# An MoE bias load on another queue, and a reordered end, in a decoder layer

## The chip, the cores and the metric

The kernel runs on one core of a Trainium2 chip, and the metric is the device time of one execution in microseconds (us). Inside the core, TensorE (PE; its weight loads are PEld), VectorE (DVE), ScalarE (ACT), GpSimd (POOL) and SyncE (SP) each work through a list of their own and wait for each other by semaphores. DMAs are issued by SP and ACT, each from its place in its list, and are carried out by 16 DMA engines that the core has.

## The reference

One decoder layer on 256 tokens of width 1024, all in float32: a mixer with three branches, a LayerNorm, a mixture of experts, a LayerNorm. The change touches the mixture of experts alone:

```
logits = xf @ router_w + router_b
top_v, top_i = lax.top_k(logits, 4)            # 4 of 32 experts for each token
gates = jax.nn.softmax(top_v, axis=-1)
...
def expert_block(xblk, e):
    h = xblk @ w1[e] + b1[e]                   # (., 1024) @ (1024, 2048)
    gate, upv = jnp.split(h, 2, axis=-1)
    gate = jnp.minimum(gate, 7.0); upv = jnp.clip(upv, -7.0, 7.0)
    act = (upv + 1.0) * (gate * jax.nn.sigmoid(1.702 * gate))
    return act @ w2[e] + b2[e]                 # (., 1024) @ (1024, 1024)
...
y = sum over a token's experts of gate * expert_block
x = layer_norm(ALPHA * x + y, ln2_g, ln2_b)
```

The weights of one expert are 12 MB (8 MB of `w1`, 4 MB of `w2`), so 384 MB over 32 experts. The second bias `b2` is 32 x 1024 numbers, 128 KB in all.

## The kernel before, in words

The mixer comes first. Then a loop goes over the experts e = 0 to 30, and the last one, 31, is written out behind it. Each expert works on up to 64 tokens, which a matmul with a matrix of zeros and ones gathers into a token buffer: there are three, `xg[0]` to `xg[2]`, used in turn (expert e uses `xg[e % 3]`), and `xg[2]` lies in the tile `rws`. For an expert, `gemm1` makes the first product into the PSUM tiles `h`, copied into `hs` (in tile `t`) by ACT and DVE; `act_steps` transposes `hs` on PE, adds the first bias while it empties PSUM into `hT`, and then makes the activation `a` with DVE and one sigmoid on ACT. `gemm2` makes the second product from `a`, ACT copies it into `ys`, and `scatter` adds it, weighted by the gates, to four PSUM tiles `acc` that hold the sum over all experts. The loop runs these staggered: within the body of expert e stand gemm1 and act of e, gemm2 of e-1, and scatter of e-2 or e-1. The second bias enters once for all: `gated_biases` adds the gates (transposed, tile `GT`) times the rows of `b2` to `acc`, four products of 512 columns.

The weights stream through a ring of 23 buffers of 1 MB (`new_w`, tile `w`). `load_w` (L75) issues one load of 1 MB from SP: eight for a `w1`, four for a `w2`. Program order of the loads is: `w1` of expert 0; then for each e, `w1` of e and `w2` of e-1. The last expert's weights are loaded by a class `Last` with some pieces of 512 KB (L1157). The loads are issued from SP's list as far ahead of their use as two things allow: a free buffer of the ring (a wait for PE), and a free semaphore. The framework below the kernel gives every DMA of SP's and ACT's queues, in the order of the program's text, the next of eight semaphores, DMAHW0 to DMAHW7; a DMA waits for the one that held its semaphore before, whichever queue that was on.

In the kernel before, `b2` is loaded by SP in the body of expert 30 into a ring buffer of its own (L1291), and `gated_biases` stands in that body, between the transposes of act and the rest of it. `gates_by_expert` makes `GT` in the body of expert 8. Experts with more than 64 tokens would be finished after the loop by `overflow`, a branch that is taken only when the largest count is above 64.

Of the kernel before, what the change touches and what calls it, by code (L numbers as in the profile page):

```python
# [19 lines left out]
D = 1024  # L20
# [31 lines left out]
def hybrid(ctx: ExitStack, tc: tile.TileContext, A, out, dbg=None):  # L52
# [967 lines left out]

    hs = t1[:, :1024]
    hT = t1[:, 1024:].rearrange("p (j h s) -> p j h s", j=8, h=2)
    wblk = rws.rearrange("p v k e -> p (v k e)")
# [66 lines left out]
    def gemm1(xg, w1):  # L1090

        hp = [h_tile(c) for c in range(2)]
        for k, c, half in w1.order:
            PE.matmul(hp[c][half * 64:(half + 1) * 64], xg[:, k],
                             w1(k, half * 2 + c), start=(k == 0), stop=(k == 7), skip_group_check=True)
        nc.scalar.copy(hs[:, :512], hp[0])  # L1096
        nc.vector.tensor_copy(hs[:, 512:], hp[1])  # L1097

    class Weights:


        def __init__(self, e, one=False):
            self.e, self.one = e, one
            self.order = ([(k, c, half) for c in range(2) for half in range(2) for k in range(8)] if one else
                          [(k, c, half) for k in range(8) for c in range(2) for half in range(2)])

        def block(self, name, k, c):
            cs = slice(c * 512, (c + 1) * 512)
            if name == 'moe_w1':
                src = A[name][ds(self.e, 1), k * 128:(k + 1) * 128, cs]  # L1110
            else:
                src = w2v[ds(self.e, 1), :, k // 2, k % 2, cs]
            nc.sync.dma_start(wblk, src.rearrange("e p f -> p (e f)"))
            return wblk

    class First(Weights):
        def load(self):
            self.w = [load_w(w1v[self.e][:, k:k + 1, :], 1, 2048) for k in range(8)]
            return self

        def __call__(self, k, c):
            if self.one:
                return self.block('moe_w1', k, c)
            return self.w[k][:, 0, c * 512:(c + 1) * 512]

    class Second(Weights):
        def load(self):
            self.w = [load_w(w2v[self.e][:, q], 2, 1024) for q in range(4)]
            return self

        def __call__(self, k, c):
            if self.one:
                return self.block('moe_w2', k, c)
            return self.w[k // 2][:, k % 2, c * 512:(c + 1) * 512]

    class Last:
# [26 lines left out]
                PE.matmul(hp[c][h * 64:(h + 1) * 64], xg[(E - 1) % 3][:, k], w,  # L1163
                          start=(k == 0), stop=(k == 7), skip_group_check=True)

        def second(self, yp, j, c):

            for h in range(2):
                PE.matmul(yp[c][h * 64:(h + 1) * 64, :256], a_main[:, j],
                          self.w2[j // 2][:, j % 2, h * 512 + c * 256:h * 512 + (c + 1) * 256],  # L1170
                          start=(j == 0), stop=(j == 7), skip_group_check=True)

    def act_steps(bias, a, g=None, banks=None):


        bv = bias.rearrange("p (h j) -> p j h", h=2)
        pieces = [slice(q * 4, (q + 1) * 4) for q in range(2)]
        js = slice(0, 8)
        if g is not None:
            js = slice(4 * g, 4 * g + 4)  # L1180
            pieces = [js]
        for i, piece in enumerate(pieces):
            n = piece.stop - piece.start
            p = (banks[i] if banks else u_tile())[:, :n * 128]
            for j in range(n):
                PE.transpose(p[:, j * 128:(j + 1) * 128], pair(hs, piece.start + j), ident)
            nc.vector.tensor_tensor(hT[:, piece], p.rearrange("p (j h s) -> p j h s", j=n, h=2),  # L1187
                                    bv[:, piece, :].unsqueeze(3).to_broadcast([128, n, 2, SLOTS]), op=OP.add)
        yield
        gate, up = hT[:, js, 0, :], hT[:, js, 1, :]  # L1190
        nc.vector.tensor_scalar(gate, gate, LIMIT, None, op0=OP.min)
        sg = hs[:, js.start * 128:js.start * 128 + (js.stop - js.start) * 64].rearrange("p (j s) -> p j s", s=64)
        nc.scalar.activation(sg, gate, AF.Sigmoid, scale=1.702)
        nc.vector.tensor_scalar(up, up, LIMIT, -LIMIT, op0=OP.min, op1=OP.max)
        nc.vector.tensor_tensor(sg, sg, gate, op=OP.mult)
        nc.vector.scalar_tensor_tensor(a[:, js], up, 1.0, sg, op0=OP.add, op1=OP.mult)  # L1196

    def act(*args, **kw):
        for _ in act_steps(*args, **kw):
# [2 lines left out]

    def gemm2(a, w2):
        yp = u_tile()
        for k, c, half in w2.order:
            if c == 0:
                PE.matmul(yp[half * 64:(half + 1) * 64, :], a[:, k], w2(k, half),
                                 start=(k == 0), stop=(k == 7), skip_group_check=True)
        nc.scalar.copy(ys, yp)  # L1209

    def scatter(gT, first=False):
# [7 lines left out]
    def gates_by_expert():  # L1219
        p = u_tile()[:E, :T]  # L1220
        for t in range(2):
            PE.transpose(p[:, t * 128:(t + 1) * 128], G[:, t, :], ident)
        GT = lp.tile([E, T], F32, name="GT")
        nc.vector.tensor_copy(GT, p)
        return GT

    def gated_biases(GT, b2r):
        for t in range(2):
            for h in range(2):
                PE.matmul(acc[t][h], GT[:, t * 128:(t + 1) * 128], b2r[:, h * 512:(h + 1) * 512],  # L1230
                                 start=False, stop=False, skip_group_check=True)

    def overflow(stores):

# [4 lines left out]
        with tc.If(most > SLOTS):  # L1239
            with tc.For_i(0, E, 1) as ei:  # L1240
                ce = nc.values_load(cnts[0:1, ds(ei, 1)], min_val=0, max_val=T)
                with tc.If(ce > SLOTS):
                    be = lp.tile([128, 16], F32, name="be")
                    nc.vector.tensor_copy(be.unsqueeze(2), b1T[:, :, ds(ei, 1)])
                    gev = lp.tile([128, 2, 1], F32, name="gev")
                    nc.vector.tensor_copy(gev, G[:, :, ds(ei, 1)])
                    rke = lp.tile([128, 2, 1], F32, name="rke")
                    nc.vector.tensor_copy(rke, rk[:, :, ds(ei, 1)])
                    with tc.For_i(1, T // SLOTS, 1):
                        nc.vector.tensor_scalar(rke, rke, float(SLOTS), None, op0=OP.subtract)  # L1250
# [3 lines left out]
                        gemm1(xg[0], First(ei, True))  # L1254
                        a = act(be, xg[0])
                        gemm2(a, Second(ei, True))
                        scatter(gT)
            st = row_sums()
            for c in range(2):
# [22 lines left out]
    for e in range(E - 1):  # L1282
# [3 lines left out]
        w1 = First(e).load()  # L1286
        if 0 < e < E - 2:
            w2 = Second(e - 1).load()
        if e == E - 2:
            b2r = new_w()[:E, :D]  # L1290
            nc.sync.dma_start(b2r, A['moe_b2'])  # L1291
        if e:
            weigh(gates(e), buf)
            if e == E - 2:
# [15 lines left out]
        elif e < E - 2:  # L1310
# [13 lines left out]
            if odd:  # L1324
                gT = turn_slots(buf, h_tile(0))
                find(e + 1, 1, u_tile())
            late = prev[1], e == 1
            if e == SUMS:
                scatter(*late)
                late = None  # L1330
                residuals()
                GT = gates_by_expert()
# [28 lines left out]
    steps = [act_steps(b1T[:, :, E - 1], a_main, c) for c in range(2)]  # L1361
    yp = []
    for c in range(2):
        for k in (6, 7):
            last.first(banks, k, c)
        nc.scalar.copy(hs[:, c * 512:(c + 1) * 512], banks[c])
        if c:
            yp.append(h_tile(0))
            for j in (0, 1):
                last.second(yp, j, 0)  # L1370
        next(steps[c])
        for _ in steps[c]:
            pass
    yp.append(h_tile(1))
    for j in range(6):
        for c in range(2):
            if j > 1 or c:
                last.second(yp, j, c)

    def row_sums():  # L1380
        return [lp.tile([128, 4, 6], F32, name=f"st{t}") for t in range(2)]
# [7 lines left out]
    for c in range(2):  # L1389
        cs = slice(c * 256, (c + 1) * 256)  # L1390
        for j in (6, 7):
            last.second(yp, j, c)
        nc.scalar.copy(ys[:, cs], yp[c][:, :256])  # L1393
        for t in range(2):
            for h in range(2):
                r = slice(h * 64, (h + 1) * 64)
# [4 lines left out]
    y = new_w().rearrange("p (t d) -> p t d", t=2)  # L1401

    def normed(st):
        stats = [statistics(st[t]) for t in range(2)]
# [48 lines left out]
```

## Time and profile before

| | |
|---|---|
| device time, median of 3 runs (range) | 1202.81 us (1200.18 to 1204.87) |
| the profiled execution: its own time, its span | 1199.88 us, 1198.0 us |
| PE busy | 1134.0 us (95% of the span) |
| DVE, ACT, POOL busy | 347.0, 208.2, 64.4 us |
| bytes read from HBM | 447.25 MB, 374 GB/s over the span |

The span goes from the first to the last instruction of the profiled execution; about 1.9 us of its time lie around it. The profile cuts the span in 40 equal slices, and from the tenth on it shows the DMA engines filled.

### The profile page before, as it was taken

How to read it: one execution, taken by the hardware profiler on the slowest of the kernel's cores; microseconds unless marked ns; L12 is line 12 of the kernel's file. 1: busy time of each engine (PE TensorE's matmuls, PEld its weight loads, DVE VectorE, ACT ScalarE, POOL GpSimd, SP SyncE). 2: the span in 40 equal slices, each digit the busy share in tenths (PEclk: the TensorE clock that was granted, in tenths of full speed). 3: DMA queues.
4: the chain of work that ended last, by engine and by line, in shares of the span. 5: the costliest groups of instructions: out<-in, count | busy, mean ns of one | idle time of the engine just before them, and what ended most of it. 6: DMA issues, size and time to landing. Idle time of an engine off the chain costs nothing.

```text
span 1198.0 us, 15607 instructions
## 1 busy us (share of the span) xinstructions
PE 1134.0 (95%) x6464; PEld 584.8 (49%) x6465; DVE 347.0 (29%) x700; ACT 208.2 (17%) x491; POOL 64.4 (5%) x106
## 2 busy tenths in 40 slices
PE   8999999999999999999999898989898989899994
PEld 7998889984434334343433333333333333334332
DVE  6679777472112111111121111111111111111014
ACT  5115554532101011010101000101010101011001
POOL 1010001311000000000000000000000000000000
PEclk9999999999999999999999999999999999999998
DMA  9994466869999999999999999999999999999993
GB/s 247 327 321 142 129 205 250 306 231 419 424 424 424 424 425 423 425 423 425 423 425 422 426 423 425 423 424 423 426 423 425 424 424 425 425 424 425 419 406 153
DMA packets 100358, 449.37 MB, mean 375 GB/s; under 512 B 11108, under 2 KB 44826, under 8 KB 51514
## 3 DMA queue, kind: packets, MB, share of 16 engines
q1 hardware_dynamic: 99774, 447.51, 92.6%
q8 instruction: 52, 0.85, 0.3%
q10 hardware_dynamic: 508, 0.81, 0.2%
q14 instruction: 24, 0.20, 0.1%
HBM read 447.25 MB, written 1.05 MB: 374 GB/s over the span
## 4 chain that ended last, share of the span: by engine, by line
DMA 51%; PE 45%; DVE 2%; SPq 1%; ACT 1%; issue 0%; ACTq 0%; DVEq 0%
DMA w<-in_moe_w_dram 50%; PE h L48 16%; PE u L48 8%; PE mm L87 4%; PE mm L88 4%; PE mm L89 4%; PE acc L48 3%; DMA w<-in_w_in_dram 1%; PE sc L641 1%; PE yps L686 1%; PE ptp L677 1%; PE sc L48 1%; PE mm L48 1%; DVE w L48 0%; DMA x<-in_x_dram 0%
## 5 line engine op out<-in xcount | busy, mean ns | idle before, releaser
L48 PE MATMUL h<-w,t 128*64 128x512 f32 (+1 forms) x1472 | 328.0, 588 | 31.2 <-DMA w<-in_moe_w_dram 30.4
L48 PEld LDWEIGHTS h<-w,t 128*64 128x64 f32 x1472 | 99.4, 136 | 249.0 <-issue 161.4
L48 PE MATMUL u<-w,t 128*64 128x512 f32 x960 | 212.9, 595 | 0.0
L1097 DVE COPY t<-h 128x512 f32<-128x512 f32 x31 | 21.4, 691 | 512.8 <-PE h L48 512.8
L48 PE MATMUL h<-w,rws 128*64 128x512 f32 x640 | 146.2, 603 | 11.2 <-DMA w<-in_moe_w_dram 11.0
L48 PEld LDWEIGHTS u<-w,t 128*64 128x64 f32 x960 | 66.2, 137 | 124.4 <-issue 118.3
L48 PEld LDWEIGHTS h<-w,rws 128*64 128x64 f32 x640 | 43.8, 138 | 108.7 <-issue 76.1
L87 PE MATMUL mm<-xh,ws 128*128 128x256 f32 x336 | 96.8, 288 | 0.0
L1096 ACT COPY t<-h 128x512 f32<-128x512 f32 x31 | 18.1, 585 | 447.5 <-PE h L48 447.5
L88 PE MATMUL mm<-xl,ws 128*128 128x256 f32 x336 | 95.0, 283 | 0.0
L89 PE MATMUL mm<-xh,ws 128*128 128x256 f32 x336 | 94.9, 283 | 0.0
L82 DVE TENSOR_TENSOR ws<-w,ws 128x1024 fp32r<-128x1024 f32 (+1 forms) x64 | 73.2, 1148 | 11.8 <-ACT ws L81 11.0
L1074 POOL TENSOR_TENSOR ext<-ext,G 128x128 f32<-128x128 f32 x62 | 27.1, 456 | 815.8 <-PE h L48 797.2
L48 PE MATMUL acc<-t,ext 64*128 64x512 f32 (+1 forms) x264 | 63.9, 602 | 1.6 <-ACT t L1393 0.9
L87 PEld LDWEIGHTS mm<-xh,ws 128*128 128x128 f32 x336 | 64.3, 191 | 1.0 <-issue 0.8
L88 PEld LDWEIGHTS mm<-xl,ws 128*128 128x128 f32 x336 | 64.4, 192 | 0.0
L89 PEld LDWEIGHTS mm<-xh,ws 128*128 128x128 f32 x336 | 64.3, 191 | 0.0
L1196 DVE SCALAR_TENSOR_TENSOR t<-t 128x512 f32<-128x512 f32 (+1 forms) x32 | 21.6, 675 | 144.0 <-PE u L48 143.8
L1209 ACT COPY t<-u 128x512 f32<-128x512 f32 x31 | 18.2, 586 | 175.3 <-PE u L48 175.3
L1187 DVE TENSOR_TENSOR t<-u,b1T 128x512 f32<-128x512 f32 x35 | 24.0, 690 | 78.3 <-PE u L48 78.3
L48 PEld LDWEIGHTS acc<-t,ext 64*128 64x128 f32 x264 | 22.7, 186 | 41.1 <-issue 27.8
L81 DVE CAST ws<-w 128x1024 fp32r<-128x1024 f32 (+1 forms) x47 | 29.7, 642 | 23.0 <-PE mm L89 15.6
(338 smaller groups left out, 1085.6 us busy)
## 6 DMA issues: line engine op xcount, KB each, us to landing
w<-in_moe_w_dram SPq DMA_DIRECT2D x381, 1024.0 KB
w<-in_w_in_dram SPq DMA_DIRECT2D x22, 1024.0 KB
w<-in_w_up_dram SPq DMA_DIRECT2D x6, 1024.0 KB
w<-in_cmp_w_dram SPq DMA_DIRECT2D x4, 1024.0 KB
w<-in_w_o_dram SPq DMA_DIRECT2D x4, 1024.0 KB
w<-in_w_in_dram SPq DMA_DIRECT2D x6, 512.0 KB
w<-in_moe_w_dram SPq DMA_DIRECT2D x6, 512.0 KB
out_dram<-w SPq DMA_DIRECT2D x3, 256.0 KB
```

Of the source, the lines that this page charges most:

```text
L48: return lambda *a, **k: self.tc.keep_in_program_order(f(*a, **k))
L81: copy(hi, src)
L82: return sub.tensor_tensor(lo, src, hi.bitcast(F32), op=OP.subtract).ins
L87: pe.matmul(p, ah, bh, start=first, stop=False, **kw)
L88: pe.matmul(p, ah, bl, start=False, stop=False, **kw)
L89: pe.matmul(p, al, bh, start=False, stop=last, **kw)
L1074: nc.gpsimd.tensor_tensor(SG[:, t], S[:, t, x:x + 1].to_broadcast([128, 2, SLOTS]), gsrc[:, t].unsqueeze(2).to_broadcast([128, 2, SLOTS]), ...
L1096: nc.scalar.copy(hs[:, :512], hp[0])
L1097: nc.vector.tensor_copy(hs[:, 512:], hp[1])
L1187: nc.vector.tensor_tensor(hT[:, piece], p.rearrange("p (j h s) -> p j h s", j=n, h=2), bv[:, piece, :].unsqueeze(3).to_broadcast([128, n, ...
L1196: nc.vector.scalar_tensor_tensor(a[:, js], up, 1.0, sg, op0=OP.add, op1=OP.mult)
L1209: nc.scalar.copy(ys, yp)
```

## The change

`b2` no longer passes through the ring. In the body of expert 2, once `gemm1` has read `xg[2]`, two loads of 64 KB on ACT's queue (`load_biases`) put its two column halves into partitions 0 to 31 and 32 to 63 of that token buffer. `gated_biases` moves to the body of expert 3, ahead of the gather that refills `xg[2]`, and makes `GT` itself from a doubled copy of the gates, so that both halves have their gates on the right partitions. In expert 30, all eight transposes of act come ahead of the scatter, and the activation is made in two halves. In expert 31 the products of rows 0 to 5 (of 8) of `w2` run over 512 columns and not twice over 256, and the second half of the activation is made in two parts. The loads of the crowded branch, which were 256 KB each through one buffer, become loads of 1 MB through the ring. The final result is built in `t1` and not in a ring buffer.

```
-        for k, c, half in w1.order:
+        for k in range(8):
+            for c in range(2):
+                for half in range(2):
...
-        def second(self, yp, j, c):
+        def second(self, yp, j, cs):
...
+        for i in range(len(parts)):
+            vec.tensor_scalar(gate[i], gate[i], LIMIT, None, op0=OP.min)
+            nc.scalar.activation(sg[i], gate[i], AF.Sigmoid, scale=1.702)
+            vec.tensor_scalar(up[i], up[i], LIMIT, -LIMIT, op0=OP.min, op1=OP.max)
+        for i, js in enumerate(parts):
+            vec.tensor_tensor(sg[i], sg[i], gate[i], op=OP.mult)
+            vec.scalar_tensor_tensor(a[:, js], up[i], 1.0, sg[i], op0=OP.add, op1=OP.mult)
...
+    def load_biases(dst):
+        for h in range(2):
+            ACT.dma_start(dst[h * E:(h + 1) * E], A['moe_b2'][:, h * 512:(h + 1) * 512])
+    def gated_biases(b2r):
+        GT = lp.tile([128, T], F32, name="GT")
+        twice = GT[:, :4 * E].rearrange("p (t h e) -> p t h e", t=2, h=2)
+        nc.vector.tensor_copy(twice, G[:, :, None, :].to_broadcast([128, 2, 2, E]))
+        p = u_tile()[:2 * E, :T]
+        for t in range(2):
+            PE.transpose(p[:, t * 128:(t + 1) * 128], twice[:, t].rearrange("p h e -> p (h e)"), ident)
+        nc.vector.tensor_copy(GT[:2 * E], p)
         for t in range(2):
             for h in range(2):
-                PE.matmul(acc[t][h], GT[:, t * 128:(t + 1) * 128], b2r[:, h * 512:(h + 1) * 512],
-                                 start=False, stop=False, skip_group_check=True)
+                r = slice(h * E, (h + 1) * E)
+                PE.matmul(acc[t][h], GT[r, t * 128:(t + 1) * 128], b2r[r], start=False, stop=False,
+                          skip_group_check=True)
...
-        if e == E - 2:
-            b2r = new_w()[:E, :D]
-            nc.sync.dma_start(b2r, A['moe_b2'])
...
             steps = act_steps(b1T[:, :, e], a, banks=[u_tile(), h_tile(0)])
             next(steps)
+            if e == 3:
+                gated_biases(b2r)
...
             late = prev[1], e == 1
+            if e == 2:
+                b2r = xg[2].rearrange("p k s -> p (k s)")
+                load_biases(b2r)
...
             gT = turn_slots(buf, u_tile())
+            a = a_main
+            steps = [act_steps(b1T[:, :, e], a, c, DVE) for c in range(2)]
+            for c in range(2):
+                next(steps[c])
             scatter(prev[1])
-            steps = act_steps(b1T[:, :, e], a_main)
-            next(steps)
             gTn = turn_slots(1 - buf, h_tile(0), S)
-
-            gated_biases(GT, b2r)
-            for _ in steps:
-                pass
-            a = a_main
+            for c in range(2):
+                for _ in steps[c]:
+                    pass
```

Three places of the built program show what moves. The first is SP's list where the loads of expert 3 begin; each row is one load of 1 MB, `w1` of expert 3 from the first row on, with the semaphores that it waits for (PE's is that of the free buffer). Before:

```order
L75 DMA w<-in_moe_w_dram 128x2048 [waits DMAHW7_49,PE_49]
L75 DMA w<-in_moe_w_dram 128x2048 [waits DMAHW0_49,PE_49]
L75 DMA w<-in_moe_w_dram 128x2048 [waits DMAHW1_49,PE_49]
L75 DMA w<-in_moe_w_dram 128x2048 [waits DMAHW2_49,PE_49]
L75 DMA w<-in_moe_w_dram 128x2048 [waits DMAHW3_49,PE_49]
L75 DMA w<-in_moe_w_dram 128x2048 [waits DMAHW4_49,PE_49]
L75 DMA w<-in_moe_w_dram 128x2048 [waits DMAHW5_49,PE_49]
L75 DMA w<-in_moe_w_dram 128x2048 [waits DMAHW6_49,PE_49]
```

The same eight loads, the 33rd to the 40th of the weight stream, in the changed kernel:

```order
L75 DMA w<-in_moe_w_dram 128x2048 [waits DMAHW1_49,PE_49]
L75 DMA w<-in_moe_w_dram 128x2048 [waits DMAHW2_49,PE_49]
L75 DMA w<-in_moe_w_dram 128x2048 [waits DMAHW3_49,PE_49]
L75 DMA w<-in_moe_w_dram 128x2048 [waits DMAHW4_49,PE_49]
L75 DMA w<-in_moe_w_dram 128x2048 [waits DMAHW5_49,PE_49]
L75 DMA w<-in_moe_w_dram 128x2048 [waits DMAHW6_49,PE_49]
L75 DMA w<-in_moe_w_dram 128x2048 [waits DMAHW7_49,PE_49]
L75 DMA w<-in_moe_w_dram 128x2048 [waits DMAHW0_49,PE_49]
```

The turn of the semaphores has moved by two: DMAHW7 and DMAHW0, which the 33rd and 34th load had, are now those of the 39th and 40th. The second place is ACT's list in the body of expert 2: the copies of `hs` and of a turned gate matrix, the sigmoid, the copy of `ys`, and the copy of `hs` of expert 3. Before:

```order
L1096 COPY t_3268<-h_3664 128x512 [waits DVE_49,PE_49]
L1087 COPY ext<-h_3716 128x256 [waits PE_49]
L1193 ACTIVATE t_3268<-t_3268 128x512 [waits DVE_49,Activation_49]
L1209 COPY t_3267<-u 128x512 [waits PE_49]
L1096 COPY t_3268<-h_3770 128x512 [waits DVE_49,PE_49]
```

The same place in the changed kernel:

```order
L1097 COPY t_3268<-h_3664 128x512 [waits DVE_49,PE_49]
L1086 COPY ext<-h_3716 128x256 [waits PE_49]
L1186 ACTIVATE t_3268<-t_3268 128x512 [waits DVE_49,Activation_49]
L48 DMA rws<-in_moe_b_dram 32x512 [waits DMAHW7_49]
L48 DMA rws<-in_moe_b_dram 32x512 [waits DMAHW0_49]
L1203 COPY t_3267<-u 128x512 [waits PE_49]
L1097 COPY t_3268<-h_3772 128x512 [waits DVE_49,PE_49]
```

The two loads of `b2` stand behind the sigmoid of expert 2 and hold DMAHW7 and DMAHW0. The third place is PE's list in expert 30, from the transpose of the gates behind gemm1 (first row) to gemm2 (last row). Before:

```order
L48 MATMUL u<-ident,ext 128x128 x2
L48 MATMUL acc_3275<-t_3267,ext 128x512
L48 MATMUL acc_3276<-t_3267,ext 128x512
L48 MATMUL acc_3466<-t_3267,ext 128x512
L48 MATMUL acc_3467<-t_3267,ext 128x512
L48 MATMUL u<-ident,t_3268 128x128 x8
L48 MATMUL h_7042<-ident,ext 128x128 x2
L48 MATMUL acc_3275<-w,GT 128x512
L48 MATMUL acc_3276<-w,GT 128x512
L48 MATMUL acc_3466<-w,GT 128x512
L48 MATMUL acc_3467<-w,GT 128x512
L48 MATMUL u<-w,t_3267 64x512 x16
```

The same place in the changed kernel:

```order
L48 MATMUL u<-ident,ext 128x128 x2
L48 MATMUL u<-ident,t_3268 128x128 x8
L48 MATMUL acc_3275<-t_3267,ext 128x512
L48 MATMUL acc_3276<-t_3267,ext 128x512
L48 MATMUL acc_3466<-t_3267,ext 128x512
L48 MATMUL acc_3467<-t_3267,ext 128x512
L48 MATMUL h_7047<-ident,ext 128x128 x2
L48 MATMUL u<-w,t_3267 64x512 x16
```

The eight transposes of act stand ahead of the scatter, and the four products with `GT` are gone from here; they stand in expert 3, behind the transposes of its act.

## Rows read from the trace of the kernel before

**Rows 1.** The page: span, DMA rate in 40 slices, loads of expert weights.

```profile
span 1198.0 us, 15607 instructions
...
GB/s 247 327 321 142 129 205 250 306 231 419 424 424 424 424 425 423 425 423 425 423 425 422 426 423 425 423 424 423 426 423 425 424 424 425 425 424 425 419 406 153
...
w<-in_moe_w_dram SPq DMA_DIRECT2D x381, 1024.0 KB
...
w<-in_moe_w_dram SPq DMA_DIRECT2D x6, 512.0 KB
```

**Rows 2.** Stretches: length, busy time by engine, PE clock, DMA share, GB/s.

```profile
263.00:345.00 82.00, 81.25 (x471) 39.30 (x471) 22.72 (x61) 14.57 (x31) 7.59 (x12) 1.00 1.00 412
345.00:531.00 186.00, 185.19 (x924) 75.38 (x921) 30.36 (x53) 18.90 (x42) 6.33 (x14) 1.00 1.01 424
531.00:1130.00 599.00, 559.53 (x2704) 212.05 (x2705) 85.86 (x150) 57.87 (x127) 18.26 (x42) 1.00 1.01 424
1130.00:1142.00 12.00, 9.77 (x44) 2.82 (x42) 0.61 (x1) 0.84 (x2) 0.00 (x0) 1.00 1.02 392
```

**Rows 3.** The chain of work that ended last: start, us, what.

```profile
531.66 1.56 PE h L48 x7
533.23 19.71 DMA w<-in_moe_w_dram
...
1139.40 1.94 PE h L48 x8
```

**Rows 4.** Waits of SP's queue, whole span: us in total, times, longest.

```profile
SPq L75 <- DMA w<-in_moe_w_dram: 673.4, 325, 2.9
```

**Rows 5.** Waits of SP's queue, 1139.9 to 1140.5 us.

```profile
SPq L75 <- DMA w<-in_moe_b_dram: 0.3, 1, 0.3
```

**Rows 6.** SP's issues in order: start, length to the last one's end, count.

```profile
194.04 58.30 SPq L75 DMA_DIRECT2D w<-in_moe_w_dram  x17
263.29 41.57 SPq L75 DMA_DIRECT2D w<-in_moe_w_dram  x21
306.25 0.33 SPq L75 DMA_DIRECT2D w<-in_moe_w_dram  x1
311.44 28.39 SPq L75 DMA_DIRECT2D w<-in_moe_w_dram  x14
341.22 3.76 SPq L75 DMA_DIRECT2D w<-in_moe_w_dram  x3
346.55 0.33 SPq L75 DMA_DIRECT2D w<-in_moe_w_dram  x1
...
1121.54 0.33 SPq L1291 DMA_DIRECT2D w<-in_moe_b_dram  x1
```

**Rows 7.** ACT in order of time, expert 2; idle before in brackets.

```profile
335.92 0.37 ACT L1087 COPY ext<-h 128x256 f32<-128x256 f32 x1 [3.55 <-PE h L48]
337.50 0.63 ACT L1193 ACTIVATE t<-t 128x512 f32<-128x512 f32 x1 [1.21 <-DVE t L1191]
342.95 0.58 ACT L1209 COPY t<-u 128x512 f32<-128x512 f32 x1 [4.82 <-PE u L48]
```

**Rows 8.** Stretches at the issue of a 1 MB load to idle DMA engines.

```profile
255.00:263.00 8.00, 8.00 (x43) 6.83 (x42) 6.75 (x13) 0.29 (x1) 3.00 (x2) 1.00 0.14 58
265.29:266.29 1.00, 1.00 (x11) 1.00 (x11) 0.60 (x3) 0.29 (x1) 0.00 (x0) 1.00 1.06 442
```

**Rows 9.** PE in order of time, expert 3.

```profile
342.73 13.90 PE L48 MATMUL h<-w,t 128*64 128x512 f32 x64
```

**Rows 10.** PE in order of time, experts 30 and 31.

```profile
1144.93 3.69 PE L48 MATMUL acc<-w,GT 32*128 32x512 f32 x8
...
1182.53 1.08 PE L48 MATMUL h<-w,t 128*64 128x256 f32 x8
```

**Rows 11.** Stretches at the end of the weight stream.

```profile
1178.00:1180.00 2.00, 2.00 (x22) 1.24 (x20) 0.13 (x1) 0.00 (x0) 0.00 (x0) 1.00 0.36 126
1180.00:1182.00 2.00, 1.53 (x14) 0.89 (x12) 0.00 (x0) 0.37 (x1) 0.00 (x0) 1.00 0.01 3
```

More of the change, by code (lines that the diff above doesn't have):

```diff
@@ L1092, in gemm1 @@
         hp = [h_tile(c) for c in range(2)]
-        for k, c, half in w1.order:
-            PE.matmul(hp[c][half * 64:(half + 1) * 64], xg[:, k],
-                             w1(k, half * 2 + c), start=(k == 0), stop=(k == 7), skip_group_check=True)
+        for k in range(8):
+            for c in range(2):
+                for half in range(2):
+                    PE.matmul(hp[c][half * 64:(half + 1) * 64], xg[:, k],
+                              w1(k, half * 2 + c), start=(k == 0), stop=(k == 7), skip_group_check=True)
@@ L1096, in gemm1 @@
         nc.scalar.copy(hs[:, :512], hp[0])
         nc.vector.tensor_copy(hs[:, 512:], hp[1])
[L1099 to L1114, printed above, removed]
@@ L1116, in hybrid, with of_expert, __init__ @@
-    class First(Weights):
+    def of_expert(v, e):
+        return v[e] if isinstance(e, int) else v[ds(e, 1)].rearrange("e p r f -> (e p) r f")
+    class First:
+        def __init__(self, e):
+            self.src = of_expert(w1v, e)
         def load(self):
-            self.w = [load_w(w1v[self.e][:, k:k + 1, :], 1, 2048) for k in range(8)]
+            self.w = [load_w(self.src[:, k:k + 1, :], 1, 2048) for k in range(8)]
             return self
         def __call__(self, k, c):
-            if self.one:
-                return self.block('moe_w1', k, c)
@@ L1124, in __call__, with __init__ @@
             return self.w[k][:, 0, c * 512:(c + 1) * 512]
-    class Second(Weights):
+    class Second:
+        def __init__(self, e):
+            self.src = A['moe_w2'][e] if isinstance(e, int) else A['moe_w2'][ds(e, 1)].rearrange("e f d -> (e f) d")
+            self.src = self.src.rearrange("(q p r) d -> q p r d", p=128, r=2)
         def load(self):
-            self.w = [load_w(w2v[self.e][:, q], 2, 1024) for q in range(4)]
+            self.w = [load_w(self.src[q], 2, 1024) for q in range(4)]
@@ L1186, in act_steps @@
                 PE.transpose(p[:, j * 128:(j + 1) * 128], pair(hs, piece.start + j), ident)
-            nc.vector.tensor_tensor(hT[:, piece], p.rearrange("p (j h s) -> p j h s", j=n, h=2),
+            vec.tensor_tensor(hT[:, piece], p.rearrange("p (j h s) -> p j h s", j=n, h=2),
                                     bv[:, piece, :].unsqueeze(3).to_broadcast([128, n, 2, SLOTS]), op=OP.add)
         yield
[L1190 to L1196, printed above, removed]
+        n = (js.stop - js.start) // parts
+        parts = [slice(j, j + n) for j in range(js.start, js.stop, n)]
+        gate, up = [[hT[:, js, i, :] for js in parts] for i in range(2)]
+        sg = [hs[:, js.start * 128:js.start * 128 + n * 64].rearrange("p (j s) -> p j s", s=64) for js in parts]
+        for i in range(len(parts)):
[5 more added lines that the diff above has]
+            vec.scalar_tensor_tensor(a[:, js], up[i], 1.0, sg[i], op0=OP.add, op1=OP.mult)
     def act(*args, **kw):
@@ L1204, in gemm2 @@
         yp = u_tile()
-        for k, c, half in w2.order:
-            if c == 0:
+        for k in range(8):
+            for half in range(2):
                 PE.matmul(yp[half * 64:(half + 1) * 64, :], a[:, k], w2(k, half),
-                                 start=(k == 0), stop=(k == 7), skip_group_check=True)
+                          start=(k == 0), stop=(k == 7), skip_group_check=True)
         nc.scalar.copy(ys, yp)
@@ L1253, in overflow @@
                         gT = turn_slots(2, u_tile())
-                        gemm1(xg[0], First(ei, True))
+                        gemm1(xg[0], First(ei).load())
                         a = act(be, xg[0])
-                        gemm2(a, Second(ei, True))
+                        gemm2(a, Second(ei).load())
                         scatter(gT)
@@ L1331, in hybrid @@
                 residuals()
-                GT = gates_by_expert()
             if e == E - 3:
@@ L1360, in hybrid @@
             scatter(prev[1])
-    steps = [act_steps(b1T[:, :, E - 1], a_main, c) for c in range(2)]
-    yp = []
     for c in range(2):
@@ L1367, in hybrid @@
         if c:
-            yp.append(h_tile(0))
+            yp = h_tile(0)
             for j in (0, 1):
[L1370 to L1378, printed above, removed]
+                last.second(yp, j, slice(0, 512))
+        act(b1T[:, :, E - 1], a_main, c, DVE, parts=2 - c)
+    for j in range(2, 6):
+        last.second(yp, j, slice(0, 512))
     def row_sums():
@@ L1391, in hybrid @@
         for j in (6, 7):
-            last.second(yp, j, c)
-        nc.scalar.copy(ys[:, cs], yp[c][:, :256])
+            last.second(yp, j, cs)
+        nc.scalar.copy(ys[:, cs], yp[:, cs])
         for t in range(2):
@@ L1400, in hybrid @@
     ov = out[0].rearrange("(t p) d -> p t d", p=128)
-    y = new_w().rearrange("p (t d) -> p t d", t=2)
+    y = t1.rearrange("p (t d) -> p t d", t=2)
     def normed(st):
```

16 lines of the change are left out of this document (3 added, 13 removed).

## The prediction

> **What bounds the kernel now.** I read the page first, for the rate of the DMAs: from the tenth slice on they move some 424 GB/s without a pause until the last two [rows 1]. Then the stretches: 412 GB/s from 263 to 345 us, 424 from 345 to 531 and 424 from 531 to 1130, with the DMA engines' share at 1.00 to 1.01 in all three [rows 2]. A share of 1.01 means that none of the 16 engines has time left over. Third the chain of waits, which seems to say something else: up to 531 us it runs over PE, and only from 533 on over the weight loads [rows 3]. Both are true. Up to 531 PE works off a backlog of loaded weights, so no matmul waits for a load; yet the loads themselves were never slower than the engines allow. So the end is set by the weight stream: its start at 263 us, its bytes, and whatever pauses it has. A pause before 531 us costs PE nothing at that moment and the end everything, since no later stretch runs under full rate and could make it good.
>
> Fourth, what SP waits for: 325 times, and 673.4 us in all, a load's issue waits for the landing of another load [rows 4]. That is the turn of the eight semaphores: at most eight DMAs are under way, and the next waits for the eighth before it. The proof that this holds for a DMA which has nothing to do with the waiting load is at 1140 us: a weight load waits 0.3 us for the landing of the `b2` load [rows 5], which nothing in it reads; it is the eighth issue behind it.
>
> **The change, part by part.**
>
> *`b2` on ACT's queue.* In the changed lists the two `b2` loads hold DMAHW7 and DMAHW0 behind the 32nd weight load, and the 39th and 40th weight load wait for them. When does SP come to the 39th? The weight loads are issued as 17 from 194.04 us, 21 from 263.29, and one at 306.25 [rows 6]: the one at 306.25 is the 39th. When does ACT come to `b2`? Behind the sigmoid of expert 2, which runs from 337.50 to 338.13; before it ACT sits idle for DVE and PE, behind it until 342.95 [rows 7]. SP runs ahead of PE by a ring, ACT by nothing, and the change ties the one to the other. So SP is to stand at the 39th load from 306.25 until `b2` has landed.
>
> Landing: the trace has no 64 KB load to idle engines. The nearest row is the load issued at 263.29 to engines that had gone almost idle (58 GB/s in the 8 us before): 2.0 us later they move 442 GB/s [rows 6, 8]. A 64 KB load should land about when its bytes first move, so I take 2.0 us; the bounds are 1 us and the 4.5 that this 1 MB load needs with its own 2.47 us of transfer (1.0486 MB at 424 GB/s). That gives 338.2 + 2.0 = 340.2 us. If ACT's sequencer issues at the start of the sigmoid and not at its end, it is 0.6 less. The 39th load then goes out, and its bytes flow another 2.0 us later, at 342.2; it lands at 344.7.
>
> When did it land before? From 345 us on SP is at the limit of eight: 39 + 14 + 3 = 56 loads are out by then, and the 57th goes out at 346.55 [rows 6]; so the 49th landed at 346.5, and ten landings of 2.47 us earlier the 39th, at 321.8. The stream is therefore dry from 319.3 to 342.2, and everything behind it lands 344.7 - 321.8 = **22.9 us** later. Bounds by the landing price: 21.3 (1 us, and 0.6 for the sigmoid) to 25.4.
>
> What covers it? Not the queue: the 38 loads issued by then are through at 319.3. Not the ring: PE holds weights enough to go on (its first product of expert 3 starts at 342.73 and takes 1.74 us for each of eight steps, so it comes to the 39th load at 353.2, over 8 us after that has landed [rows 9]); the backlog hides the pause from PE then, and PE meets the loads earlier than at 531 us. And the `b2` bytes themselves fall in the pause.
>
> *`b2` leaves the end of the stream.* 128 KB are 0.3 us at 424 GB/s; around it the rate drops to 392 for 12 us, 0.9 us lost [rows 2]. Gain between 0.3 and 1.2, I take 0.7, for the loads of the last two experts behind it.
>
> *`gated_biases` to expert 3.* Eight matmul passes, 3.69 us [rows 10], leave expert 30 and come to expert 3 with one wait for a DVE copy of `GT` ahead, which I bound by as much again. There PE has the backlog, and the loads come 22.9 us late anyway: 0 at the end. Without that cover it is 3.7 to 7.4 us.
>
> *The end.* PE runs almost without a gap through experts 30 and 31, so 3.69 us less and transposes ahead of the scatter would let gemm2 start some 3 us sooner. But the weights stop it: data flows at 126 GB/s until 1180 us [rows 11], and the last piece's product starts at 1182.53 [rows 10]. The gain here cannot pass that 2.5 us; as the steps between (copy, transposes, activation) still follow the landing of `w1`'s last pieces one by one, I take 0, that is, PE keeps its distance to the loads. The 512-column products move the same columns in half the passes, hidden likewise.
>
> *The rest.* 381 loads of 1 MB and six of 512 KB are 384 MB [rows 1], which is 12 MB for each of 32 experts, so the crowded branch was not taken and its loads cost 0. The doubled copy of the gates and building the result in `t1` lie beside other work: 0, at most 0.5 us.
>
> Sum: 22.9 - 0.7 = +22.2 us on the profiled execution's 1199.88 us (its span and 1.9 around it), 1222.1. The median of the runs is 1202.81, 2.9 above that execution, and the change is compared with it: **1225 us**.
>
> **A rule against it.** The Trainium skill (Trainium Kernel Development and Optimization, Key Constraints) says that DMAs from SP, ACT and POOL run on the same 16 engines and interleave, and that issuing from several engines saves no more than the sequencers' issue time. By that the move of `b2` would be nearly free, and the time that of the first rival. The rule speaks of the engines; [rows 4, 5] show the tie between the queues ahead of them, at the issue.
>
> **The rivals.**
>
> *Not slower: the pause does not come, or is absorbed.* In favour: the chain runs over PE until 531 us [rows 3], as if loads had slack there. If the 39th load does not wait for `b2`, what is left is the gain at the end, 0.7 to 3.2 us: 1200 to 1202. It is decided at one place, SP's issue at 306.25. Absorbed it could only be if the engines had spare time later, and [rows 2] show none. The 0.3 us in [rows 5] are the strongest fact against. Chance 0.07, at 1202.
>
> *A short pause.* ACT's sequencer might run ahead of the copies and the sigmoid that wait for PE and DVE, and issue `b2` before them, when the semaphores allow, around 318 us. `b2` would land at 320, the 39th load's bytes flow at 322.3, and 3 us are lost: 1205. Against it: a copy of `hs` in front waits for PE's product, which still reads the buffer that `b2` overwrites, so the order has to hold. Chance 0.04.
>
> *A longer one.* PE, 4 to 7 us later from expert 3 on, becomes the bound on top of the pause, or the stream restarts more slowly than at 263 us. 1225 + 5 = 1230. Against it: PE is working off a backlog until 531 us [rows 3], so it is the faster of the two, and loads that come later only give it time. Chance 0.06.
>
> The forecast has the remaining 0.83.
>
> **How the numbers follow.** The likeliest case has 21.3 to 25.4 us for the pause, less 0.3 to 3.2 at the end, and the runs of one kernel differ by some 2 us from their median: 1220 to 1229. The range holds 8 in 10 if it reaches a little into the longer pause: 1219 to 1231. 0.5% are 6 us, about what a measurement of this kernel can tell from no change. Slower by more: the forecast and the longer pause, 0.89. Within: 0.07 x 0.9 and the short pause, 0.10. Faster by more, which needs over 6 us where the end offers 3: 0.01.
>
> **What the profile will show.** In SP's waits a row for the landing of `b2`, once, about 34 us, at L75. In the page's DMA rate two low slices: with a span of 1220 a slice is 30.5 us, the eleventh (305 to 335) near 200 GB/s, the twelfth near 330. ACT issues both `b2` loads at about 338 us. The chain turns from PE to loads well before 531 us. From 345 on the DMA engines stay at 424 GB/s. PE has `acc<-rws,GT` at about 361 us and none at the end, and the last product follows the last weights by 2 to 3 us. The prediction is wrong if SP issues the 39th load near 306 us, if ACT issues `b2` much before 337, or if the end of the weight stream moves by less than 20 us.

## The result, and the profile after

The changed kernel takes 1221.25 us (median of 4 runs, 1220.5 to 1221.4) against 1202.78 for the kernel before in the same series (4 runs, 1200.18 to 1204.87): ratio 1.016, 95% interval 1.0147 to 1.0174. It is slower by 18.5 us by these medians, inside the forecast range. Its profiled execution took 1221.4 us with a span of 1219.6, 21.6 above the span of before; the working had +22.2.

The page of the changed kernel, span and DMA rate, beside [rows 1]:

```profile
span 1219.6 us, 15565 instructions
...
GB/s 242 328 317 147 121 208 271 313 229 421 182 339 425 425 422 425 422 424 424 425 424 424 424 424 425 424 425 423 425 423 424 424 424 423 425 424 425 425 417 177
```

In a line that otherwise reads as before, two slices have fallen: the eleventh to 182 GB/s, the twelfth to 339. That is a hole in the weight stream, and the stretches give its edges (columns as in [rows 2]):

```profile
263.00:318.00 55.00, 54.24 (x340) 29.21 (x339) 19.16 (x55) 11.59 (x25) 6.96 (x9) 1.00 0.96 400
318.00:345.00 27.00, 27.00 (x135) 10.55 (x135) 4.47 (x9) 2.99 (x7) 1.38 (x4) 1.00 0.16 56
345.00:531.00 186.00, 181.00 (x873) 71.80 (x870) 27.36 (x48) 17.00 (x37) 5.32 (x12) 0.99 1.01 424
...
1201.00:1203.00 2.00, 1.97 (x10) 0.77 (x12) 0.00 (x0) 0.00 (x0) 0.00 (x0) 1.00 0.38 125
```

From 318 to 345 us the engines move 56 GB/s; at 424 they would have needed 3.6 us for those bytes, so 27 x (424 - 56) / 424 = 23.4 us of stream are gone. PE is busy for 27.00 of the same 27.00 us: it feels nothing. From 345 on the rate is 424 as before, and nothing is made good there. The stream's last two microseconds, 126 GB/s from 1178 to 1180 in [rows 11], are now 125 GB/s from 1201 to 1203: some 23 us later.

Who made the hole is in two views. First the waits of SP's queue over the whole span (us in total, times, longest), beside [rows 4]:

```profile
SPq L75 <- DMA w<-in_moe_w_dram: 694.2, 334, 3.5
SPq L75 <- DMA rws<-in_moe_b_dram: 34.6, 1, 34.6
```

A weight load has waited once for the landing of `b2`, for 34.6 us. Then ACT in order of time, beside [rows 7], and SP's issues:

```profile
338.21 0.63 ACT L1186 ACTIVATE t<-t 128x512 f32<-128x512 f32 x1 [1.21 <-DVE t L1185]
338.24 0.79 ACTq L48 DMA_DIRECT2D rws<-in_moe_b_dram  x2
```

```profile
305.27 0.33 SPq L75 DMA_DIRECT2D w<-in_moe_w_dram  x1
...
340.22 0.80 SPq L75 DMA_DIRECT2D w<-in_moe_w_dram  x2
```

The 38th weight load goes out at 305.27 and the 39th, by the tie, not before 340.22. `b2` went out at 338.24, as the sigmoid starts, and had landed 2.0 us later, when the 39th goes out.

The chain of waits (start, us, what), beside [rows 3]:

```profile
376.40 12.05 PE h L48 x55
388.45 19.73 DMA w<-in_moe_w_dram
```

It leaves PE for the loads at 388 us and not at 533: the backlog that covered the loads before is used up 145 us sooner. This is where PE first feels the pause of 318 to 342.

### The profile page after: what moved, and what is told of

Read it like the earlier page. It is cut to its first block, busy times and chain, and to the rows that moved or that the text cites. A ratio compares the mean times of both kernels' runs of the same rounds, so it can differ in the third digit from the quotient of the medians.

```text
span 1219.6 us, 15565 instructions
## 1 busy us (share of the span) xinstructions
PE 1145.0 (94%) x6440; PEld 584.0 (48%) x6441; DVE 347.6 (29%) x709; ACT 208.6 (17%) x493; POOL 64.1 (5%) x106
## 4 chain that ended last, share of the span: by engine, by line
DMA 65%; PE 32%; DVE 2%; ACT 0%; issue 0%; SPq 0%; ACTq 0%; DVEq 0%
DMA w<-in_moe_w_dram 63%; PE h L48 9%; PE mm L87 4%; PE mm L88 4%; PE mm L89 4%; PE u L48 4%; DMA w<-in_w_in_dram 1%; PE acc L48 1%; PE sc L641 1%; PE yps L686 1%; PE mm L48 1%; DVE t L48 1%; PE ptp L677 1%; PE sc L48 1%; PE ptp L48 0%; DMA x<-in_x_dram 0%
## 5 line engine op out<-in xcount | busy, mean ns | idle before, releaser
L48 PE MATMUL h<-w,t 128*64 128x512 f32 x1448 | 332.5, 597 | 36.9 <-DMA w<-in_moe_w_dram 35.5
L48 PEld LDWEIGHTS h<-w,t 128*64 128x64 f32 x1448 | 96.2, 136 | 262.7 <-issue 156.2
L48 PE MATMUL h<-w,rws 128*64 128x512 f32 x640 | 149.7, 610 | 15.8 <-DMA w<-in_moe_w_dram 15.5
L1190 DVE SCALAR_TENSOR_TENSOR t<-t 128x512 f32<-128x512 f32 x29 | 20.1, 692 | 150.4 <-PE u L48 150.4
L1186 ACT ACTIVATE t<-t 128x512 f32<-128x512 f32 (+2 forms) x35 | 20.7, 593 | 93.1 <-DVE t L1185 84.7
```

Source lines behind the costliest of these rows:

```text
L48: return lambda *a, **k: self.tc.keep_in_program_order(f(*a, **k))
L1186: nc.scalar.activation(sg[i], gate[i], AF.Sigmoid, scale=1.702)
L1190: vec.scalar_tensor_tensor(a[:, js], up[i], 1.0, sg[i], op0=OP.add, op1=OP.mult)
```

## Experiments

Three theories were to be told apart: (1) SP waits at the 39th load, by the turn of the semaphores, for `b2` from ACT, and the engines run dry; (2) packets of a second queue disturb the stream; (3) the moved products or the other edits cost the time. Each kernel was timed in one series with the kernel before; the medians of both stand with each ratio. Differences between kernels of two series, as those to the changed kernel, carry the scatter of both (the median of before was 1202.78, 1201.43, 1201.29 and 1201.88 us in four series).

**1. The same loads on SP's queue.** From the changed kernel, `b2` at the same place of the program, but issued by SP into a ring buffer:

```
-            ACT.dma_start(dst[h * E:(h + 1) * E], A['moe_b2'][:, h * 512:(h + 1) * 512])
+            tc.keep_in_program_order(nc.sync.dma_start(dst[h * E:(h + 1) * E], A['moe_b2'][:, h * 512:(h + 1) * 512]))
...
-                b2r = xg[2].rearrange("p k s -> p (k s)")
+                b2r = new_w()[:, :512]
```

> The changed kernel, but SP issues the two b2 loads itself, at the same place of the program (between the 32nd and the 33rd weight load), into a ring buffer. Theory 1 (SP waits at the 39th weight load until ACT has issued b2, and the DMA engines run dry): a queue that holds its own semaphores cannot wait for another engine's place, so no pause; the weight stream pays 0.3 to 0.9 us for the b2 bytes and the end keeps its gain of 0 to 2.5: 1198 to 1202 us, 20 us under the changed kernel. Theory 2 (b2 on a second queue disturbs the weight stream by its packets): also near 1200, since the second queue is gone. Theory 3 (the products with GT and the other edits cost the 20 us, not the load): stays at 1219 to 1222.

Measured: 1202.73 us (12 runs) against 1201.43, ratio 1.0012 (1.0003 to 1.0021). The 34 us wait is gone, and with it most of the loss, but not all: the kernel lies 0.7 us above the range expected of theory 1. Its waits of SP's queue between 300 and 370 us, and its stretches:

```profile
SPq L75 <- PE acc L48: 17.4, 1, 17.4
```

```profile
318.00:345.00 27.00, 27.00 (x134) 10.40 (x134) 4.46 (x8) 2.84 (x7) 1.23 (x4) 1.00 1.01 426
345.00:365.00 20.00, 18.99 (x98) 8.02 (x95) 3.66 (x7) 1.21 (x2) 0.00 (x0) 1.00 0.86 349
```

The stretch of the hole is full (426 GB/s). In its place stands a small wait of another kind: the ring buffer that holds `b2` comes free only with the products of expert 3 (`acc`), and the load that is to take it waits 17.4 us. 20 x (424 - 349) / 424 = 3.5 us of stream are lost, about what the kernel lies above experiment 2.

**2. The same queue, later in the program.** From the changed kernel:

```
-            if e == 3:
+            if e == 21:
                 gated_biases(b2r)
...
-            if e == 2:
+            if e == 20:
                 b2r = xg[2].rearrange("p k s -> p (k s)")
                 load_biases(b2r)
```

> The changed kernel with both steps moved from experts 2 and 3 to experts 20 and 21: b2 still comes on ACT's queue into the same token buffer, the same two semaphores are held. Theory 1: there PE has no backlog, SP is only eight loads ahead of the landings, and the 255th weight load, which is tied to b2, is issued at 838.7 us in the kernel before, 0.6 us after the sigmoid of expert 20 begins. SP waits some 2 us, with 17 us of loads under way, so no pause: 1198 to 1202 us. Theory 2: the same two loads on the same queue cost the same wherever they are: 1219 to 1222. Theory 3: the same too, 1219 to 1222.

Measured: 1199.12 us (11 runs) against 1201.43, ratio 0.9982 (0.9972 to 0.9991). Faster than before. The waits of its SP queue:

```profile
SPq L75 <- DMA rws<-in_moe_b_dram: 2.8, 2, 2.0
```

The tie is still there, but by expert 20 SP is no longer a ring ahead: it waits 2.0 us at the longest, while six loads are under way. A second queue as such (theory 2) and the products and the end (theory 3) cost nothing that can be measured, since all of them are in this kernel.

**3. The wait alone.** The kernel before, with two loads that nothing uses, in expert 2; the computation is unchanged:

```
+            if e == 2:
+                spare = xg[2].rearrange("p k s -> p (k s)")
+                for h in range(2):
+                    ACT.dma_start(spare[h * E:(h + 1) * E], A['moe_b2'][:, h * 512:(h + 1) * 512])
```

> The kernel before with one thing added: two loads of b2 on ACT's queue into the third token buffer in expert 2, which nothing reads; b2 still comes by SP in expert 30 and is used there, and none of the other edits is in. Theory 1: the load alone makes the pause, 22 to 23 us: 1221 to 1226 us by the median of before, about 1222 in the profile. Theory 3: no change, 1200 to 1204.

Measured: 1226.18 us (4 runs) against 1201.43, ratio 1.0201 (1.0185 to 1.0217). The waits of its SP queue, the stretch of the hole, and PE and its clock near the end:

```profile
SPq L75 <- DMA rws<-in_moe_b_dram: 34.4, 1, 34.4
```

```profile
318.00:345.00 27.00, 27.00 (x137) 10.68 (x137) 4.65 (x9) 3.17 (x8) 1.56 (x4) 1.00 0.16 60
...
1173.00:1182.00 9.00, 9.00 (x35) 2.86 (x36) 0.00 (x0) 0.16 (x1) 0.00 (x0) 0.81 1.01 420
```

```profile
1169.39 3.69 PE L48 MATMUL acc<-w,GT 32*128 32x512 f32 x8
1173.01 8.78 PE L48 MATMUL u<-w,t 128*64 128x512 f32 x32
```

Two loads of 64 KB that nothing waits for, except by the turn of the semaphores, make the kernel 24.8 us slower, at the upper end of the 1221 to 1226 expected. That is the pause of the changed kernel, 22.1 us, and 2.7 more. 1.7 of these are in the last row: 32 passes took 8.78 us here and 7.09 at the same place of the changed kernel and of the kernel before, and the granted clock here is 0.81 from 1173 to 1182. The other 1.0 is less than the scatter: the interval goes from 22 to 26 us, and one of the four runs took 1223.86.

**4 and 5. How the price grows with the wait.** As experiment 2, with the load in expert 5 and the products in 6, and with 8 and 9.

> The changed kernel with the two steps in experts 5 and 6. A middle dose for theory 1: here ACT's list has b2 behind the gather's copies of expert 5 (about 423 us), the tied load is the 78th, and the 77th lands at 416 us by the kernel before. b2 lands at 425, bytes of the 78th flow at 427: a pause of 11 us, give or take 2, and 1209 to 1213 us. Theories 2 and 3: 1219 to 1222 as in the changed kernel.

> The changed kernel with the two steps in experts 8 and 9, near the point from which theory 1 gives no pause. By the kernel before, the sigmoid of expert 8 begins at 493.4 us, b2 would land at 495.4, and bytes of the tied 111th load flow at 497.4; the 110th lands at 498.2. So SP waits some 14 us for b2, as much as eight loads under way just cover: pause 0 to 1 us, 1198 to 1201 us. If the wait of SP as such cost time, and not the dry engines, it would be 1208 to 1214.

Measured: expert 5, 1210.27 us (4 runs) against 1201.43, ratio 1.0073 (1.0059 to 1.0088); expert 8, 1201.32 us (10 runs) against 1201.29, ratio 0.9996 (0.9986 to 1.0005). The first lies in its range, the second 0.3 us above the 1198 to 1201 expected. Waits of SP's queue and the stretch of the hole, with the load in expert 5:

```profile
SPq L75 <- DMA rws<-in_moe_b_dram: 23.9, 2, 23.5
```

```profile
410.00:430.00 20.00, 20.00 (x112) 9.62 (x110) 3.43 (x6) 2.67 (x7) 1.01 (x2) 1.00 0.42 165
```

and in expert 8:

```profile
SPq L75 <- DMA rws<-in_moe_b_dram: 15.1, 1, 15.1
```

```profile
496.00:502.00 6.00, 5.32 (x25) 1.68 (x22) 0.69 (x1) 0.58 (x1) 0.00 (x0) 1.00 0.38 125
```

In the first, 20 x (424 - 165) / 424 = 12.2 us of stream are missing, and the kernel is 11.1 us above experiment 2. In the second 6 x (424 - 125) / 424 = 4.2 us are missing, and it is 2.2 us above (2.4 by the spans). So waits of 34.6, 23.5 and 15.1 us cost 22.1, 11.1 and 2.2 us, the wait less 12.4 to 12.9; and the wait of 2.0 us in experiment 2 itself costs nothing against experiment 8 below, which has none (1199.12 and 1199.24 us).

An estimate comes near to this. Two of the eight semaphores are `b2`'s, so six loads are under way when the wait begins, at most 6 x 2.47 = 14.8 us of work; behind it the stream needs 2.0 us to flow again: wait - 12.8. That it fits so well is in part luck. In the changed kernel the wait begins at 305.6 us, and the rate falls from 426 GB/s between 316 and 317 to 336 and then 49 between 318 and 319: the engines run dry 12.4 us after its start, and not 14.8. The stretches accordingly lose more, 23.4, 12.2 and 4.2 us, which is the wait less 10.9 to 11.3; and the end pays 1.1 to 2.0 us less than the stretches lose. Where these come back no run isolates. Theory 1 had counted eight loads as under way, and so put the price in expert 8 a little too low. It had also let `b2` land there 2.0 us after its issue, as on idle engines; issued at 493.90, with the engines still busy, it let the tied load go only at 499.25.

**6 and 7. The end and `b2` apart.** Experiment 6 is the kernel before with the end alone changed: transposes ahead of the scatter and activation in halves in expert 30, products by 512 columns in expert 31, while `b2` and its products stay in expert 30. Experiment 7 is experiment 2 with the end of the kernel before. In short, the end's edit (6 has it, 7 has not):

```
+            steps = [act_steps(b1T[:, :, e], a, c, DVE) for c in range(2)]
+            for c in range(2):
+                next(steps[c])
             scatter(prev[1])
...
-                last.second(yp, j, 0)
+                last.second(yp, j, slice(0, 512))
```

> The kernel before with the edits of the end alone: in expert 30 the transposes ahead of the scatter and the activation in two halves, in expert 31 the 512-column products and the activation in parts; b2 still by SP in expert 30, with its four products there. If the 2 us by which the run with both steps in experts 20 and 21 beats the kernel before come from the order at the end, this keeps most of them: 1199 to 1200.5 us. If they come from b2 and its products leaving the end, it is 1201 to 1202.

> The other half: the end as in the kernel before, but b2 on ACT's queue in expert 20 and its products in expert 21. If the 2 us come from b2 and its products (3.69 us of PE) leaving the end: 1199 to 1200; if from the order at the end: 1201 to 1202. No pause in either.

Measured: the end alone, 1201.63 us (11 runs) against 1201.29, ratio 1.0003 (0.9994 to 1.0012); `b2` alone, 1200.18 us (11 runs) against 1201.29, ratio 0.9989 (0.9979 to 0.9999). The reordered end alone is worth nothing that can be measured; `b2` alone falls between the two ranges expected. PE from the last step of gemm1 to gemm2 (first and last row), in order of time, with the end alone:

```profile
1138.95 1.94 PE L48 MATMUL h<-w,t 128*64 128x512 f32 x8 [0.81 <-DMA w<-in_moe_w_dram]
...
1144.71 4.00 PE L48 MATMUL acc<-w,GT 32*128 32x512 f32 x8
1148.65 8.42 PE L48 MATMUL u<-w,t 128*64 128x512 f32 x32
```

with `b2` alone:

```profile
1140.12 1.94 PE L48 MATMUL h<-w,t 128*64 128x512 f32 x8 [0.55 <-DMA w<-in_moe_w_dram]
...
1149.08 7.09 PE L48 MATMUL u<-w,t 128*64 128x512 f32 x32 [3.36 <-issue]
```

and with both, in the changed kernel:

```profile
1162.92 1.94 PE L48 MATMUL h<-w,t 128*64 128x512 f32 x8 [0.55 <-DMA w<-in_moe_w_dram]
...
1168.93 7.09 PE L48 MATMUL u<-w,t 128*64 128x512 f32 x32 [0.19 <-PE h L48]
```

Between the two rows lie 9.7, 9.0 and 6.0 us; in the kernel before it was 9.2 (1139.40 in [rows 3], and 1148.6, the end of the products in [rows 10]). With the end alone the products with `GT` still stand between. With `b2` alone they are gone, but PE then sits idle for 3.36 us ahead of gemm2, whose activation DVE ends at 1148.98. So the 3 us or so that PE gains there need both steps together; neither gives them by itself.

**8. One word.** The changed kernel with `b2` on POOL's queue, at the same place of the program:

```
-            ACT.dma_start(dst[h * E:(h + 1) * E], A['moe_b2'][:, h * 512:(h + 1) * 512])
+            GPS.dma_start(dst[h * E:(h + 1) * E], A['moe_b2'][:, h * 512:(h + 1) * 512])
```

> The changed kernel with one word changed: the two loads of b2 stand at the same place, in expert 2, in the same buffer, but on GpSimd's queue, whose DMAs do not take a turn of the eight semaphores of SP and ACT (the 39th weight load waits for the 31st again). Theory 1: no pause, 1198 to 1202 us. If it is the time at which b2 comes, or a second queue, that costs: 1219 to 1222.

Measured: 1199.24 us (10 runs) against 1201.29, ratio 0.9982 (0.9973 to 0.9992). POOL's issue, and the stretch that held the hole:

```profile
333.68 1.22 POOL L48 DMA_DIRECT2D rws<-in_moe_b_dram  x2 [15.33 <-PE h L48]
```

```profile
318.00:345.00 27.00, 27.00 (x135) 10.40 (x135) 4.46 (x8) 2.82 (x6) 2.32 (x5) 1.00 1.01 419
```

SP's waits have no row for `b2`. POOL waits for PE before its issue, as ACT did for PE and DVE, but no weight load waits for POOL's DMA. The 39th goes out at 306.68, 27 us ahead of `b2`'s issue. The same transfer, issued some 5 us earlier than by ACT (333.68 against 338.24), costs 22 us less.

**9 and 10. What made experiments 2 and 8 faster than before.** From the start of the last product with weights to the end of the span the kernel before takes 1198.0 - 1182.53 = 15.5 us and the changed one 1219.6 - 1205.36 = 14.2; every kernel above falls into one of these two groups. Two edits of the change divide them: the place of the result, and the crowded branch's loads. Each alone on the kernel before; the first is one line, of the second the core:

```
-    y = new_w().rearrange("p (t d) -> p t d", t=2)
+    y = t1.rearrange("p (t d) -> p t d", t=2)
```

```
-                        gemm1(xg[0], First(ei, True))
+                        gemm1(xg[0], First(ei).load())
                         a = act(be, xg[0])
-                        gemm2(a, Second(ei, True))
+                        gemm2(a, Second(ei).load())
```

> The kernel before, with the final result built in t1 and nothing else changed. Of the ten traces so far, those of kernels that build it in a ring buffer have 15.4 to 15.7 us from the start of the last product with weights to the end of the span, and those that build it in t1 have 13.9 to 14.2; but all of the latter also have the crowded branch's loads of 1 MB. Theory A: the place of the result does it. Then this kernel has 13.9 to 14.2 us there and a median about 1.4 us below that of before, ratio near 0.9988. Theory B: the shorter code of the crowded branch does it. Then 15.4 to 15.7 us and a ratio of 1.000.

> The kernel before, with the loads of the crowded branch by 1 MB through the ring and nothing else changed; the branch is not taken. Theory A (the place of the result makes the end shorter): 15.4 to 15.7 us from the start of the last product with weights to the end of the span, ratio 1.000. Theory B (the branch's code does): 13.9 to 14.2 us, ratio near 0.9988. If both show about half, neither holds alone.

Measured: the result in `t1`, 1201.11 us (11 runs) against 1201.88, ratio 0.9993 (0.9984 to 1.0003), 1198.7 - 1182.97 = 15.7 us at the end; the branch, 1200.07 us (11 runs) against 1201.88, ratio 0.9986 (0.9976 to 0.9995), 1197.1 - 1182.60 = 14.5 us at the end. So it is the code of the branch, which is never taken. It accounts for 1.0 of the 1.3 to 1.5 us between the groups: 14.5 is just above the 13.9 to 14.2 expected of it, and the rest stays open. SP's waits in the last 7 us, at the branch's own line, first of the kernel before:

```profile
SPq L1239 <- SPq L1239: 2.5, 1, 2.5
```

then with the result in `t1`, and with the branch's loads by 1 MB:

```profile
SPq L1239 <- SPq L1239: 2.7, 1, 2.7
```

```profile
SPq L1229 <- SPq L1229: 1.5, 2, 1.1
```

Behind the compare that skips the branch, SP waits for nothing but itself: 2.5 us before and 1.5 with the shorter code (1.6 in the changed kernel). That this is the fetching of instructions from behind the skipped code is an inference; the view shows only where the time lies.

## Why the prediction held, point by point

**The tie.** The step "SP is to stand at the 39th load from 306.25 until `b2` has landed" held in place and size: one wait of 34.6 us where about 34 was forecast, `b2` out at 338.24, landing 2.0 us later, slices of 182 and 339 GB/s where 200 and 330 stood. Experiment 3 makes it with the loads alone, and experiment 8 takes it away with the queue alone, so the cause is shown and not only argued.

**Its price.** 22.9 us forecast. The changed kernel lies 22.1 us above experiment 2 (medians of two series; 22.6 in their profiled executions, 1221.4 and 1198.84). ACT's queue issued as the sigmoid started and not at its end, the 0.6 us that the working kept as a bound. In part the fit is luck: the stream was dry from 318 and not from 319.3, and lost 23.4 us, of which the end paid 22.1. The sentence that "no later stretch runs under full rate and could make it good" leaves out the last 8 us of the stream, which run at 357, 240, 191 and 126 GB/s in the kernel before (1172 to 1180, in steps of 2 us); the difference may have come back there, which is not shown.

**The products in expert 3.** Taken as 0, and PE shows no wait for a load there. In order of time:

```profile
360.25 0.38 PE L48 MATMUL u<-ident,GT 128*64 128x128 f32 x2
361.64 1.99 PE L48 MATMUL acc<-rws,GT 32*128 32x512 f32 x8 [1.01 <-DVE GT L1225]
363.56 3.67 PE L48 MATMUL h<-ext,x 128*128 128x128 f32 x16
```

The eight passes take 1.99 us and not the 3.69 of [rows 10], and the wait for the copy of `GT` 1.01 us. The working bounded both from above.

**The end.** This step was mis-sized. `b2` out of the stream (0.7), the end's order (0) and the crowded branch (0) made -0.7. All of them together, without the pause, are worth 2.3 us in medians (experiment 2: 0.9982, 0.9972 to 0.9991). The sentence "the crowded branch was not taken and its loads cost 0" was right on the loads and wrong on the code: with the longer code SP takes 1.0 us more to get past it, of the 2.3. That 1.0 is read from the traces; the median of experiment 10 lies 1.8 us below before, with an interval of 0.6 to 2.9. The order is 0 within its interval, as said. For `b2` and its products there remain between 0.1 us (experiment 7, 1.1, less the 1.0) and 1.3 (experiment 2 less the 1.0). The intervals of these runs overlap, so the 0.7 that was taken is neither confirmed nor refuted.

**The offset.** The sum gave 1222.1 us for the profiled execution, which took 1221.4. The other 2.9 us of the forecast were the distance of the median of before to its profiled execution, carried over to the changed kernel; there it is 0 (1221.25 against 1221.4). Three runs of a kernel that scatters by 5 us do not give such a distance: over 33 runs the median of before was 1201.29, 1.4 above that execution. In medians the forecast of 1225 is too high by 3.75, of which some 1.4 are the base (1202.81 for the 1201.43 of experiment 2's series), 0.8 the pause (22.9 for 22.1) and 1.6 the end (0.7 for 2.3). All three erred to the same side, and the range covered them.

**The rivals.** That the pause is absorbed or does not come is refuted by the hole and by experiment 3. The short pause hung on an early issue by ACT, which came at 338.24. The longer one needed PE to fall behind on top; PE meets the loads at 388 us, but the last product follows the end of the stream as forecast, within 2 to 3 us:

```profile
1205.36 1.08 PE L48 MATMUL h<-w,t 128*64 128x256 f32 x8
```

**The rule against it.** The Trainium skill (Trainium Kernel Development and Optimization, Key Constraints) says that DMAs issued from SP, ACT and POOL run on the same 16 engines, and that issuing from several engines saves only issue time. Experiments 2 and 8 agree: the move costs nothing where no load is held up by it. Experiment 3 shows what the rule leaves out, 24.8 us for two small loads on another queue, spent ahead of the engines, at the issue. One argument of the working was weaker than it looked: in [rows 4, 5] every wait is of SP's queue for SP's own loads, so they show the turn, but not that it ties two queues. That stood only in the lists of the built program, and the wait of 34.6 us is the first trace to show it.

## What to carry to other kernels

Before a DMA moves to another engine's queue, look at which completion semaphore it takes and who has the next turn on it: through a shared turn, a queue that runs far ahead is held at the program position of one that runs on time. The price at the end was here the wait less 12.4 to 12.9 us, for the most part what the loads already under way cover: a stream that runs at full rate nearly to its end has little time to make good the rest, even if the engine that uses the data feels nothing when it happens. Put such a load where the leading queue has little lead (experiment 2), or on a queue that the leading one does not wait for (experiment 8).

## What the runs showed of the hardware that was not expected

**Products of 32 rows on two groups of partitions.** Eight passes took 3.69 us with both factors on partitions 0 to 31 [rows 10] and 1.99 us with half of them on partitions 32 to 63, at a granted clock of 1.00 and 0.99. The Trainium skill (TensorE: Matmul & The Clock Gate, Why this matters for your kernels) says that products with few rows run at the same time when their operands lie on different groups of 32 partitions; these rows agree, with a ratio of 1.85 for two groups.

**Short stretches at a lower clock.** The row at 363.56 above took 3.67 us, and the same 16 passes take 2.05 us at the same place in experiment 8. The row there, and the stretch of the changed kernel around its own:

```profile
363.28 2.05 PE L48 MATMUL h<-ext,x 128*128 128x128 f32 x16
```

```profile
363.00:368.00 5.00, 5.00 (x24) 3.82 (x22) 0.39 (x1) 0.65 (x2) 0.00 (x0) 0.66 1.00 423
```

The granted clock is 0.66 over these 5 us, a mixture of 2.4 and 1.2 GHz. Ahead of it PE had been idle for 1.01 us and had run the 32-row products. They stand ahead of the slow gemm2 of experiments 3 and 6 too, but experiment 8 has them, and the same idle time, without the fall; what decides it stays open.

**A branch that is not taken has a price.** Some 1.0 us between two lengths of the skipped code, in the trace of experiment 10.
